# First attention's PSUM: three tiles of two banks in place of six of one

## The chip, the cores and the metric

One Trainium2 core runs the whole program. The metric is the device time of one execution in microseconds; lower is better. Five engines work side by side, each through its own list of instructions in a fixed order: TensorE (PE; its weight loads are shown as PEld), VectorE (DVE), ScalarE (ACT), GpSimd (POOL) and SyncE (SP, which issues the DMA). PSUM, where every matmul writes, has eight banks of 512 fp32 columns on 128 partitions.

## The reference, cut to what matters

Two transformer blocks run one after the other on 2048 tokens of width 1024. The change lies in the attention of the first block, which for each block of 128 queries scores all allowed keys with a small indexer, keeps 256 of them, and attends to these:

```python
def block(i):                       # 128 queries, 16 blocks
    allowed = key_chunk[None, :] <= q_chunk[:, None]
    logits = jnp.einsum('bqhd,bsd->bqhs', qib, ki)              # 8 index heads
    iscore = jnp.einsum('bqhs,bqh->bqs', jax.nn.relu(logits), wib)
    iscore = jnp.where(allowed[None], iscore, -jnp.inf)
    _, idx = lax.top_k(iscore, k_sel)                           # 256 keys
    ...
    s = jnp.einsum('bqgrd,bqkgd->bqgrk', qg, kg) * scale        # 8 heads, 2 key heads
    p = jax.nn.softmax(s, axis=-1)
    o = jnp.einsum('bqgrk,bqkgd->bqgrd', p, vg)
```

Around it stand an input projection, a pooling branch, two gated output projections, and a second block with a windowed attention.

## The kernel before

The program has five stages: the projections that attention needs (`phase_a`), the first attention together with the other 28 projections of the first block (`dense`), the merge of the first block, the second block's projections with its attention, and the second merge. The change touches the second stage.

**Attention in tiles.** Block `i` has `K = 128(i+1)` keys. `index_scores` walks them in chunks of 512 columns: one matmul per index head into a PSUM tile (L462), a relu in place on ACT (L465), and a multiply-add into `score` on DVE (L467, L469). `search` then finds the 256th largest score bit by bit; DVE counts (L483, L484), or ACT counts for spans up to 900 keys (L489), and POOL turns each count into the next threshold (L524, L526). Its tail (L563 to L572, on DVE and POOL) writes a `bias` per key, 0 or -1e30, into the tile `half`. `scores` makes, per head and chunk of 512 keys, two matmuls into a PSUM tile (L628) and one DVE instruction that adds the bias, writes `s` to SBUF and keeps the row's extremum (L632, followed by a read of the accumulator); then ACT takes the exponential over up to 1024 columns (L636). `sums` walks the keys two tiles of 128 at a time: four transposes of `s` (two heads) into a PSUM tile (L650), ACT rounds it to `th` (hi, L655), a matmul with minus identity takes hi off the PSUM tile (L657), ACT rounds the rest (lo, L658), and hi and lo are multiplied with the values into `po` (L664). The last of these matmuls is a mark.

**PSUM.** In this stage one bank (`acc`) takes the dense projections, one (`psO`) takes `po`, and six tiles of one bank (`psS`, also used as `psT`) take index scores, attention scores and transposes in turn. `th` has three buffers.

**Order.** Two attention blocks make a unit of 2048 keys altogether (blocks 8 and 6, 9 and 5, 10 and 4, then 15 alone, 14 and 0, 13 and 1, 12 and 2, 11 and 3, and last 7 alone). While one unit attends, the search of the next and the index scores of the one after run beside it (`attention_1`); the search is marked urgent. A scheduler that runs when the program is built lays out each engine's list. Dense matmuls (L295, 24 per output tile, evacuated by ACT at L209) are held by `paced`: after a lead of `D0` groups each group of three may start only behind a mark, so that they spread evenly over the marks; `SL` is the number of marks by which they run ahead.

Of the kernel before, what the change touches and what calls it, by code (L numbers as in the profile page):

```python
# [45 lines left out]
class Prog:  # L46
# [150 lines left out]
    hl = ()  # L197
    D0, SL = 240, 60
    pace = False
    groups = 0  # L200
    turned = []
    AK = 900
    TP, PP, BP, HW, PO = 3, 5, 3, 8, 1
    PASSES = ((0, 0), (0, 1), (1, 0))
# [53 lines left out]
    def ps(self, pool):  # L258
        return pool.tile([P, 512], F32, name="ps")

# [188 lines left out]
    def index_scores(self, x, i, off):  # L449

        nc = self.nc
        K = (i + 1) * P
        for h0 in (0, 4):
            qI = self.xp.tile([P, 4, P], F32R, name="qI")
            nc.sync.dma_start(qI.bitcast(F32), self.qid[i][:, h0:h0 + 4])
            for c0 in range(0, K, 512):
                w = min(512, K - c0)
                n = max(w, 256)
                xc = x[:, off + c0:off + c0 + w]
                for h in range(h0, h0 + 4):  # L460
                    ps = self.ps(self.psS)
                    nc.tensor.matmul(ps[:, :n], qI[:, h - h0, :], self.kI[:, c0:c0 + n], start=True, stop=True)  # L462
                    wc = self.wi[:, i, h:h + 1]
                    r = ps[:, :w]
                    nc.scalar.activation(r, r, AF.Relu)  # L465
                    if h == 0:
                        nc.vector.tensor_scalar(xc, r, wc, 0.0, op0=ALU.mult, op1=ALU.add)  # L467
                    else:
                        nc.vector.scalar_tensor_tensor(xc, r, wc, xc, op0=ALU.mult, op1=ALU.add)  # L469
                    yield w / 960.0  # L470
        nc.vector.memset(x[0:64, off + K - 64:off + K], -3.0e38)
# [129 lines left out]
    def scores(self, x, g, pr):  # L601
# [11 lines left out]
        for e in range(2):  # L613
# [8 lines left out]
            ss.append(s)  # L622
            for c0 in range(0, K, 512):
                w = min(512, K - c0)
                n = max(w, 256)
                ps = self.ps(self.psS)
                for q in (x["qA"], x["qB"]):
                    nc.tensor.matmul(ps[:, :n], q[:, 2 * pr + e, :], x["kap"](g, c0, n), start=q is x["qA"],  # L628
                                     stop=q is x["qB"])
                first = nm[:, h:h + 1] if c0 else 3.0e38 if sink is None else sink[1][:, h:h + 1]  # L630
# [8 lines left out]
    def sums(self, x, g, pr):  # L639
# [3 lines left out]
        po = self.psO.tile([P, 512], F32, name="po")  # L643
        for k0 in range(0, nkt, 2):
            m = min(2, nkt - k0)
            pt = self.ps(self.psT).rearrange("p (k e t) -> p k e t", k=2, e=2)
            for kk in range(m):
                for e in range(2):
                    c, off = divmod((k0 + kk) * P, self.CW)
                    nc.tensor.matmul(pt[:, kk, e, :], ss[e][c][:, off:off + P], self.ident.bitcast(F32), is_transpose=True,  # L650
                                     start=(kk == e == 0), stop=(kk == m - 1 and e == 1))
            th = self.tp.tile([P, 2, 2, 256], F32R, name="th")
            ptf = pt[:, :m].rearrange("p k e t -> p k (e t)")
            hi, lo = th[:, 0, :m], th[:, 1, :m]
            nc.scalar.copy(hi, ptf)  # L655
            if self.PL == "E":
                nc.tensor.matmul(ptf, self.minus, hi, start=False, stop=True, skip_group_check=True)  # L657
                nc.scalar.copy(lo, ptf)  # L658
# [452 lines left out]
    def run(self):  # L1111
# [28 lines left out]
        with ExitStack() as es:  # L1140
# [5 lines left out]
            with ExitStack() as ep:  # L1146
# [5 lines left out]
                self.projected = self.turned[-76:]  # L1152
            self.banks(es, 1, 7 - self.PO)
            self.psO = self.pl(es, "psO", self.PO, PSUM)
            self.psT = self.psS
            self.att_pools(es, 1024, self.PP, self.TP)
# [125 lines left out]
```

## Time and profile before

| what | us |
|---|---|
| median of 3 runs | 3424.64 (3421.09 to 3427.6) |
| the profiled execution | 3433.52 |
| its span in the trace | 3431.8 |
| PE busy over the span | 3185.6 (93%) |
| DVE busy | 2353.4 (69%) |
| ACT busy | 1862.0 (54%) |

A group of the profile's costliest instructions gives line, engine and operation, what is written from what, the count, the busy time, the mean length of one, and the engine's idle time before them with what ended it. A row of a table by windows gives each engine's busy time in a stretch, with the number of instructions, and then the granted TensorE clock as a share of full speed (1.00 is 2.4 GHz, 0.50 is 1.2 GHz).

### The profile page before, as it was taken

The page shows a single profiled execution, that of the slowest core. Times are in us where ns is not written, and L with a number is a line of the kernel's source. Part 1 is how long each engine was busy: PE and PEld are TensorE (multiplying, and loading weights), DVE is VectorE, ACT ScalarE, POOL GpSimd, SP SyncE. Part 2 cuts the span into 40 slices and gives each one's busy share as a digit, 9 for nine tenths or more (in the row PEclk, how much of TensorE's full clock was granted, in tenths as well). Part 3 has the DMA queues.
Part 4 walks back from the last instruction along what each step waited for, and adds up shares of the span by engine and source line. Part 5 has one row for each costly group of instructions (what it writes and reads, how often), then busy time and mean ns, then how long its engine had stood idle before and what let it go on. Part 6 is the DMA issues. An engine that isn't in the chain of part 4 may idle for free. (4 is left out here: it accounts for less than half of the span.)

```text
span 3431.8 us, 47878 instructions
## 1 busy us (share of the span) xinstructions
PE 3185.6 (93%) x15880; PEld 2642.8 (77%) x15880; DVE 2353.4 (69%) x4745; ACT 1862.0 (54%) x3498; POOL 820.6 (24%) x1293
## 2 busy tenths in 40 slices
PE   5997989999988999997889999999999999999998
PEld 5996767787766777875667878888888887777787
DVE  5875778889998888635887556446446455668765
ACT  3553676886666687663444333335444445764443
POOL 0432145522324365202322113102102111111100
PEclk9998999999988999998899999999999999999999
DMA  5657875435323443566886555445555446878654
GB/s 182 236 159 267 281 263 182 145 127 172 128 76 103 131 150 129 163 196 195 258 280 230 183 173 175 164 154 174 192 152 187 153 149 211 256 223 275 227 184 147
DMA packets 290824, 637.78 MB, mean 186 GB/s; under 512 B 46096, under 2 KB 100112, under 8 KB 276240
## 3 DMA queue, kind: packets, MB, share of 16 engines
q1 hardware_dynamic: 290576, 634.73, 56.7%
q8 instruction: 125, 2.05, 0.2%
q14 instruction: 123, 1.01, 0.1%
HBM read 467.22 MB, written 167.38 MB: 185 GB/s over the span
## 5 line engine op out<-in xcount | busy, mean ns | idle before, releaser
L295 PE MATMUL ps<-h,hl 128*128 128x512 f32 x5376 | 1372.9, 400 | 18.0 <-ACT st L209 16.6
L295 PEld LDWEIGHTS ps<-h,hl 128*128 128x128 f32 x5376 | 987.0, 189 | 227.0 <-ACT st L209 26.8
L274 PE MATMUL ps<-hl,h 128*128 128x512 f32 (+3 forms) x3840 | 821.5, 368 | 27.5 <-DVE st L899 9.8
L274 PEld LDWEIGHTS ps<-hl,h 128*128 128x128 f32 x3840 | 671.1, 191 | 126.2 <-DVE st L899 10.8
L337 DVE TENSOR_TENSOR hl<-raw,hl 128x1024 fp32r<-128x1024 f32 (+3 forms) x364 | 440.6, 1211 | 333.9 <-ACT hl L336 332.2
L336 ACT CAST hl<-raw 128x1024 fp32r<-128x1024 f32 (+4 forms) x380 | 366.4, 965 | 380.0 <-PE ps L274 143.2
L878 PE MATMUL ps<-h,hl 128*128 128x512 f32 x1536 | 384.4, 410 | 29.6 <-DVE g L880 9.2
L878 PEld LDWEIGHTS ps<-h,hl 128*128 128x128 f32 x1536 | 299.7, 197 | 104.9 <-ACT hl L336 11.6
L484 DVE SCALAR_TENSOR_TENSOR junk<-half,sm,junk 128x704 bf16<-128x704 int16 (+17 forms) x316 | 321.9, 1019 | 5.3
L524 POOL TENSOR_SCALAR sm<-sm 128x1 f32<-128x1 f32 x448 | 181.4, 408 | 591.6 <-DVE junk L484 297.4
L636 ACT ACTIVATE s<-s,nm 128x1024 f32<-128x1024 f32 (+7 forms) x320 | 237.7, 745 | 152.9 <-DVE nm L632 151.7
L650 PE MATMUL ps<-ident,s 128*128 128x128 f32 x1344 | 225.3, 279 | 34.1 <-ACT s L636 28.7
L655 ACT CAST th<-ps 128x512 fp32r<-128x512 f32 (+1 forms) x352 | 196.1, 572 | 84.2 <-PE ps L650 60.5
L650 PEld LDWEIGHTS ps<-ident,s 128*128 128x128 f32 x1344 | 167.0, 143 | 72.4 <-ACT s L636 42.1
L664 PE MATMUL po<-th,vS 128*128 128x256 f32 x1088 | 200.6, 290 | 4.0 <-ACT th L658 3.3
L469 DVE SCALAR_TENSOR_TENSOR score<-ps,wi,score 128x512 f32<-128x512 f32 (+3 forms) x266 | 177.6, 679 | 20.9 <-ACT ps L465 18.5
L664 PEld LDWEIGHTS po<-th,vS 128*128 128x128 f32 x1088 | 167.6, 190 | 30.0 <-ACT th L658 11.3
L526 POOL TENSOR_SCALAR sm<-sm 128x1 f32<-128x1 f32 x448 | 180.5, 403 | 40.0
L658 ACT CAST th<-ps 128x512 fp32r<-128x512 f32 (+1 forms) x288 | 156.9, 567 | 56.3 <-PE ps L657 55.1
L465 ACT ACTIVATE ps<-ps 128x512 f32<-128x512 f32 (+3 forms) x304 | 154.3, 534 | 56.1 <-PE ps L462 55.5
L483 DVE TENSOR_SCALAR junk<-half,sm 128x704 bf16<-128x704 int16 (+17 forms) x316 | 145.5, 460 | 48.0 <-POOL sm L526 43.3
L209 ACT COPY st<-ps 128x512 f32<-128x512 f32 x156 | 91.1, 584 | 135.5 <-PE ps L295 69.9
(278 smaller groups left out, 4049.3 us busy)
## 6 DMA issues: line engine op xcount, KB each, us to landing
hl<-wk SPq DMA_DIRECT2D x84, 1024.0 KB, 5.2
raw<-in_wu SPq DMA_DIRECT2D x140, 512.0 KB, 4.4
raw<-in_wd SPq DMA_DIRECT2D x128, 512.0 KB, 4.5
zd<-st SPq DMA_DIRECT2D x224, 256.0 KB, 2.9
g<-zd SPq DMA_DIRECT2D x128, 256.0 KB, 4.4
wk<-hl SPq DMA_DIRECT2D x28, 1024.0 KB, 4.8
qd<-qs SPq DMA_DIRECT2D x32, 512.0 KB, 5.7
qA<-qd SPq DMA_DIRECT2D x64, 256.0 KB, 3.4
```

The lines of the kernel that those rows point to most:

```text
L274: nc.tensor.matmul(ps[b][:, :n], h[k][:, s, b * P:(b + 1) * P], wt[:, r, kk, :], start=(k == 0 and i == 0), stop=(k == KT - 1 and i == 2))
L295: nc.tensor.matmul(ps, wt[:, r, k, :], h[k][:, s, :], start=(k == 0 and i == 0), stop=(k == KT - 1 and i == 2))
L336: self.nc.scalar.copy(hi, src)
L337: (eng or self.nc.gpsimd).tensor_sub(lo, src, hi.bitcast(F32))
L484: self.nc.vector.scalar_tensor_tensor(junk, x[:, h:], thr, junk, op0=op, op1=ALU.add, accum_out=out)
L524: nc.gpsimd.tensor_scalar(one(u, e), one(p, e), one(q, e), 0.5 if bit else 1.0, op0=ALU.is_ge, op1=ALU.subtract)
L526: nc.gpsimd.tensor_scalar(one(c, e), one(u, e), w, one(c, e), op0=ALU.mult, op1=ALU.add)
L636: nc.scalar.activation(p, p, AF.Exp, scale=-1.0, bias=nm[:, h:h + 1], accum_out=x["sums"][:, c, h:h + 1])
L650: nc.tensor.matmul(pt[:, kk, e, :], ss[e][c][:, off:off + P], self.ident.bitcast(F32), is_transpose=True, start=(kk == e == 0), stop=(kk = ...
L655: nc.scalar.copy(hi, ptf)
L664: last = nc.tensor.matmul(po[:, :256], x["vap"](kt, g), th[:, r, kk], start=(kt == 0 and r == 0), stop=(kt == nkt - 1 and r == 1))
L878: nc.tensor.matmul(ps, wt[:, r, 4 * e + k, :], ab[4 * e + k][:, s, :], start=(k == 0 and i == 0), stop=(k == 3 and i == 2))
```

## The change

`psS` becomes three tiles of 1024 columns, that is two banks each. Each matmul still writes 512 columns at most, so a chunk of 1024 keys takes two matmuls (or two pairs) into the halves of one tile; what ACT and DVE do with the tile they do in one instruction of up to 1024 columns. `sums` goes four key tiles at a time: eight transposes, one hi of 1024 columns, two corrections of 512, one lo of 1024. `th` doubles in size and has two buffers in place of three. There are fewer marks (one per four key tiles), and `SL` goes from 60 to 30. The second block's attention keeps its 512 columns.

```diff
-    D0, SL = 240, 60
+    D0, SL = 240, 30
+    wide = None
-    TP, PP, BP, HW, PO = 3, 5, 3, 8, 1
+    TP, PP, BP, HW = 2, 5, 3, 8
...
-        return pool.tile([P, 512], F32, name="ps")
+        return pool.tile([P, 1024 if pool is self.wide else 512], F32, name="ps")
...
-            for c0 in range(0, K, 512):
-                w = min(512, K - c0)
-                n = max(w, 256)
+            for c0 in range(0, K, 1024):
+                w = min(1024, K - c0)
...
-                    nc.tensor.matmul(ps[:, :n], qI[:, h - h0, :], self.kI[:, c0:c0 + n], start=True, stop=True)
+                    for d in range(0, w, 512):
+                        n = max(min(512, w - d), 256)
+                        nc.tensor.matmul(ps[:, d:d + n], qI[:, h - h0, :], self.kI[:, c0 + d:c0 + d + n], start=True, stop=True)
...
-            for c0 in range(0, K, 512):
-                w = min(512, K - c0)
-                n = max(w, 256)
+            for c0 in range(0, K, self.CW):
+                w = min(self.CW, K - c0)
                 ps = self.ps(self.psS)
-                for q in (x["qA"], x["qB"]):
-                    nc.tensor.matmul(ps[:, :n], q[:, 2 * pr + e, :], x["kap"](g, c0, n), start=q is x["qA"],
-                                     stop=q is x["qB"])
+                for d in range(0, w, 512):
+                    n = max(min(512, w - d), 256)
+                    for q in (x["qA"], x["qB"]):
+                        nc.tensor.matmul(ps[:, d:d + n], q[:, 2 * pr + e, :], x["kap"](g, c0 + d, n),
+                                         start=q is x["qA"], stop=q is x["qB"])
...
-        for k0 in range(0, nkt, 2):
-            m = min(2, nkt - k0)
-            pt = self.ps(self.psT).rearrange("p (k e t) -> p k e t", k=2, e=2)
+        step = self.CW // 256
+        for k0 in range(0, nkt, step):
+            m = min(step, nkt - k0)
+            pt = self.ps(self.psT).rearrange("p (k e t) -> p k e t", k=step, e=2)
...
-            th = self.tp.tile([P, 2, 2, 256], F32R, name="th")
+            th = self.tp.tile([P, 2, step, 256], F32R, name="th")
...
-                nc.tensor.matmul(ptf, self.minus, hi, start=False, stop=True, skip_group_check=True)
+                for d in range(0, m, 2):
+                    nc.tensor.matmul(ptf[:, d:min(d + 2, m)], self.minus, hi[:, d:min(d + 2, m)], start=False, stop=True,
+                                     skip_group_check=True)
...
-            self.banks(es, 1, 7 - self.PO)
-            self.psO = self.pl(es, "psO", self.PO, PSUM)
-            self.psT = self.psS
+            self.acc = self.pl(es, "acc1", 1, PSUM)
+            self.psO = self.pl(es, "psO", 1, PSUM)
+            self.psT = self.psS = self.wide = self.pl(es, "psS", 3, PSUM)
```

PE's list holds the same 15800 matmuls before and after. DVE's and ACT's lists are 384 instructions shorter each: on ACT 304 relus become 176, and 576 casts (hi and lo) of this attention become 320; on DVE 304 multiply-adds become 176, and 320 reductions, each with its read of the accumulator, become 192. The lists differ from the first index matmul on; from the merge of the first block onward they hold the same work in the same order, up to a few places near its beginning.

The first place is PE's list where block 15 takes over from blocks 10 and 4 and its first transposes, corrections and products stand. Before (L650 transposes, L657 correction, L664 products with the values, L462 index scores, L628 scores):

```order
L650 MATMUL ps<-ident,s 128x128 x9
L462 MATMUL ps<-kI,qI 128x512
L657 MATMUL ps<-th,minus 128x512
L664 MATMUL po<-th,vS 128x256
L650 MATMUL ps<-ident,s 128x128 x4
L657 MATMUL ps<-th,minus 128x512 x2
L664 MATMUL po<-th,vS 128x256 x4
L628 MATMUL ps<-kS,qA 128x512
L628 MATMUL ps<-kS,qB 128x512
```

and now (L654, L662, L670, L464 and L631 are the same five):

```order
L654 MATMUL ps<-ident,s 128x128 x7
L464 MATMUL ps<-kI,qI 128x512 x2
L654 MATMUL ps<-ident,s 128x128 x8
L662 MATMUL ps<-th,minus 128x512 x2
L670 MATMUL po<-th,vS 128x256
L631 MATMUL ps<-kS,qA 128x512
L631 MATMUL ps<-kS,qB 128x512
```

Two steps of eight transposes now stand one behind the other ahead of the first correction; in between there is no dense matmul in either list.

The second place is PE's list in the middle of the same unit, from a step's transposes to its products. Before:

```order
L650 MATMUL ps<-ident,s 128x128 x4
L295 MATMUL ps<-h,hl 128x512 x3
L628 MATMUL ps<-kS,qA 128x512
L628 MATMUL ps<-kS,qB 128x512
L664 MATMUL po<-th,vS 128x256 x3
L462 MATMUL ps<-kI,qI 128x512
L657 MATMUL ps<-th,minus 128x512
L664 MATMUL po<-th,vS 128x256
```

and now, with the dense matmuls at L296:

```order
L296 MATMUL ps<-h,hl 128x512 x18
L662 MATMUL ps<-th,minus 128x512 x2
L670 MATMUL po<-th,vS 128x256
L464 MATMUL ps<-kI,qI 128x512
L464 MATMUL ps<-kI,qI 128x256
L654 MATMUL ps<-ident,s 128x128 x8
L670 MATMUL po<-th,vS 128x256 x7
```

Work comes in longer runs of one kind: dense matmuls in a run of 18 where runs of three stood, and the next step's eight transposes between a correction and the products that need its lo.

The third place is DVE's list where the search of block 15's unit has just ended and that of blocks 14 and 0 is in its middle. Tile `half_5642` holds the bias of block 15, which is the unit that attends next; `half_6756` and `half_7815` belong to units behind it. Before:

```order
L549 SCALAR_TENSOR_TENSOR half_6756<-half_6756,sm_6759,low_7812 128x1920
L469 SCALAR_TENSOR_TENSOR score_7842<-ps_7867,wi_207,score_7842 128x512
L632 ISA s_7836,nm_7830<-ps_7838,half_5642 128x512
L632 ISA nm_7830 128x1
L537 TENSOR_SCALAR low_7820<-half_7815 128x1792
L553 TENSOR_TENSOR sm_6759<-sm_6759 128x1
```

and now, where `half_4295` is the bias of the unit that still attends (blocks 10 and 4):

```order
L551 SCALAR_TENSOR_TENSOR half_6340<-half_6340,sm_6343,low_7252 128x1920
L635 ISA s_7140,nm_6846<-ps_7141,half_4295 128x640
L635 ISA nm_6846 128x1
L635 ISA s_7157,nm_6846<-ps_7158,half_4295 128x640
L635 ISA nm_6846 128x1
L555 TENSOR_TENSOR sm_6343<-sm_6343 128x1
```

Behind the same instruction of the search (L549, now L551) DVE took up the new unit's first scores; now it has two of the old unit's scores left.

## Rows read from the trace of the kernel before

**Rows 1.** The page's first part: the span, and and per engine the busy time, its share of the span and the instructions.

```profile
span 3431.8 us, 47878 instructions
PE 3185.6 (93%) x15880; PEld 2642.8 (77%) x15880; DVE 2353.4 (69%) x4745; ACT 1862.0 (54%) x3498; POOL 820.6 (24%) x1293
```

**Rows 2.** The views of lines L462 and L664: engine, operation, count, then the shortest, median and longest instruction in ns, then the first and the last start in us.

```profile
L462 PE MATMUL ps<-kI,qI x304: 274/393/796, 336.1 to 1295.8; 128*128 128x512 f32 x112, 128*128 128x256 f32 x24, 128*128 128x384 f32 x16
...
L664 PE MATMUL po<-th,vS x1088: 274/281/416, 572.2 to 1555.7; 128*128 128x256 f32 x182
```

**Rows 3.** Busy time by windows over the stage of the first attention: window, its length, then for PE, PEld, DVE, ACT and POOL the busy us with the number of instructions, the granted TensorE clock, the share of the DMA engines, GB/s. The last row sums the four.

```profile
320.00:560.00 240.00, 222.51 (x921) 171.87 (x920) 176.36 (x357) 149.25 (x281) 81.09 (x195) 0.98 0.75 260
560.00:920.00 360.00, 346.36 (x1862) 287.26 (x1861) 316.73 (x732) 277.38 (x588) 129.04 (x294) 0.99 0.44 148
920.00:1220.00 300.00, 258.59 (x1313) 209.45 (x1312) 265.87 (x582) 199.65 (x413) 107.58 (x200) 0.90 0.31 100
1220.00:1560.00 340.00, 328.60 (x1853) 275.99 (x1852) 225.67 (x585) 241.63 (x526) 118.92 (x244) 1.00 0.52 166
sum 1240.00, PE 1156.06 PEld 944.57 DVE 984.63 ACT 867.90 POOL 436.64; mean PE 289.01 PEld 236.14 DVE 246.16 ACT 216.98 POOL 109.16
```

**Rows 4.** What PE waited for from 320 to 1560 us: the waiting line and the one that released it, us in total, times, longest.

```profile
PE ps L295 <- ACT st L209: 16.4, 24, 2.0
PE ps L462 <- DVE score L469: 15.5, 8, 8.2
PE ps L650 <- ACT s L636: 14.4, 13, 3.5
...
PE ps L657 <- ACT th L655: 7.1, 5, 5.2
PE ps L628 <- DVE nm L632: 6.6, 8, 1.7
PE ps L650 <- DVE nm L632: 3.9, 2, 3.0
PE po L664 <- ACT th L658: 3.3, 7, 0.7
```

**Rows 5.** The table by windows again (columns as in rows 3), for two stretches inside units and four short ones at their changes.

```profile
840.00:920.00 80.00, 79.72 (x462) 68.84 (x461) 75.23 (x170) 58.21 (x130) 18.41 (x55) 1.00 0.44 140
940.00:960.00 20.00, 9.90 (x20) 5.13 (x21) 19.37 (x48) 8.81 (x13) 2.30 (x3) 0.52 0.00 1
...
1060.00:1080.00 20.00, 13.98 (x53) 9.27 (x51) 16.84 (x36) 9.53 (x14) 9.54 (x6) 0.85 0.20 73
1080.00:1100.00 20.00, 15.77 (x76) 12.17 (x76) 18.95 (x47) 18.70 (x42) 9.32 (x25) 0.81 0.21 66
1180.00:1200.00 20.00, 14.48 (x70) 11.70 (x69) 14.87 (x43) 11.05 (x26) 5.52 (x4) 0.83 0.49 155
...
1340.00:1400.00 60.00, 60.00 (x351) 51.97 (x351) 49.18 (x134) 43.62 (x97) 33.02 (x60) 1.00 0.43 137
```

**Rows 6.** ACT's groups of instructions by line and shape, 320 to 1560 us: line, engine, operation, what is written from what, count, then busy us, mean ns of one, idle time before them and who ended it.

```profile
L655 ACT CAST th<-ps 128x512 fp32r<-128x512 f32 x256 | 146.8, 594 | 46.3 <-PE ps L650 24.5 <-PE po L664 21.1
L658 ACT CAST th<-ps 128x512 fp32r<-128x512 f32 x256 | 145.4, 591 | 53.8 <-PE ps L657 52.6
L465 ACT ACTIVATE ps<-ps 128x512 f32<-128x512 f32 x224 | 126.8, 587 | 42.7 <-PE ps L462 42.3
...
L655 ACT CAST th<-ps 128x256 fp32r<-128x256 f32 x32 | 12.1, 377 | 3.4 <-PE po L664 1.7 <-PE ps L650 1.6
```

**Rows 7.** DVE's groups by line and shape over the same stretch, columns as in rows 6.

```profile
L469 DVE SCALAR_TENSOR_TENSOR score<-ps,wi,score 128x512 f32<-128x512 f32 x196 | 145.0, 745 | 16.9 <-ACT ps L465 15.9
L632 DVE CUSTOM_DVE_ANT_0 s<-ps,half,nm 128x512 f32<-128x512 f32 x120 | 89.4, 746 | 32.0 <-PE ps L628 23.4 <-PE ps L650 7.0 <-issue 0.2
...
L632 DVE DVE_READ_ACCUMULATOR2_ANT nm<- 128x1 f32 x320 | 26.3, 82 | 0.0
...
L469 DVE SCALAR_TENSOR_TENSOR score<-ps,wi,score 128x256 f32<-128x256 f32 x21 | 10.0, 478 | 0.3 <-ACT ps L465 0.3
```

**Rows 8.** The timeline near 338 us, where six relus and three multiply-adds run without a gap: start in us, us from the first start to the last end, engine, line, operation, shape, count.

```profile
337.81 3.03 ACT L465 ACTIVATE ps<-ps 128x512 f32<-128x512 f32 x6
...
341.27 2.06 DVE L469 SCALAR_TENSOR_TENSOR score<-ps,wi,score 128x512 f32<-128x512 f32 x3
```

**Rows 9.** The timeline at the change from blocks 10 and 4 to block 15, in order of start; columns as in rows 8, and in brackets the engine's wait before the instruction and who ended it.

```profile
937.70 4.05 POOL L572 TENSOR_TENSOR half<-half,eq 128x2048 bf16<-128x2048 bf16 x1
...
938.33 3.69 DVE L483 TENSOR_SCALAR junk<-half,sm 128x960 bf16<-128x960 int16 x1
...
938.71 0.40 PE L628 MATMUL ps<-kS,qB 128*128 128x512 f32 x1
...
944.33 2.22 DVE L549 SCALAR_TENSOR_TENSOR half<-half,sm,low 128x1920 uint16<-128x1920 int16 x1 [0.60 <-ACT low L547]
946.47 0.74 DVE L469 SCALAR_TENSOR_TENSOR score<-ps,wi,score 128x512 f32<-128x512 f32 x1
...
947.27 0.79 PE L462 MATMUL ps<-kI,qI 128*128 128x512 f32 x1 [8.16 <-DVE score L469]
...
955.01 0.47 PE L650 MATMUL ps<-ident,s 128*128 128x128 f32 x1 [1.81 <-ACT s L636]
```

More of the change, by code (lines that the diff above doesn't have):

```diff
@@ L650, in sums @@
                     nc.tensor.matmul(pt[:, kk, e, :], ss[e][c][:, off:off + P], self.ident.bitcast(F32), is_transpose=True,
-                                     start=(kk == e == 0), stop=(kk == m - 1 and e == 1))
-            th = self.tp.tile([P, 2, 2, 256], F32R, name="th")
+                                     start=(kk % 2 == e == 0), stop=(e == 1 and (kk % 2 == 1 or kk == m - 1)))
+            th = self.tp.tile([P, 2, step, 256], F32R, name="th")
             ptf = pt[:, :m].rearrange("p k e t -> p k (e t)")
```

## The prediction

> **What bounds the kernel now.** I read the first part of the page, then the tables by windows over the changed stage, then PE's waits there, and last the timeline at one bad place. The page shows PE busy for 3185.6 of 3431.8 us [rows 1], so a gain has to come out of PE's idle time or out of its clock. The changed work runs from the first index matmul at 336 us to the last product with the values at 1556 us [rows 2]. From 320 to 1560 us PE is busy for 1156.1 of 1240 us, DVE for 984.6, ACT for 867.9 [rows 3]: 84 us of PE idleness. The clock column adds to that: 0.98 over 240 us, 0.99 over 360 and 0.90 over 300 mean 4.8, 3.6 and 30 us lost, 38 us together. No change that leaves PE's work alone can give more than 84 + 38 = 122 us here.
>
> The reader should see where this sits. Inside a unit PE is full: 79.7 of 80 us from 840, with DVE at 75.2, and 60.0 of 60 from 1340, with DVE at 49.2 [rows 5]. The loss sits at the changes of unit: 10.1 us of PE idleness from 940 to 960 at a clock of 0.52, then 6.0, 4.2 and 5.5 us in the stretches at 1060, 1080 and 1180, at 0.85, 0.81 and 0.83 [rows 5]. That is 25.8 us of idleness and (0.48 + 0.15 + 0.19 + 0.17) x 20 = 19.8 us of clock, 45.6 us in 80. The clock is at full speed in the full stretches and falls in those with pauses; it follows the waits.
>
> At 938.7 us PE had run out of what it may start. Its next index matmul waited 8.16 us for a PSUM tile to be freed by a multiply-add on DVE, and DVE reached this at 946.5, behind search work: a count of 3.69 us beside POOL's 4.05 us product, and a 2.22 us instruction that waited for ACT [rows 9]. After that the new unit has to fill up: its first transpose comes at 955.0 [rows 9]. Dense matmuls could not fill the pause, since they wait for marks and no mark falls there.
>
> **The change part by part.** *PE* keeps its 15800 matmuls of the same shapes: 0.
>
> *ACT* drops 384 instructions. Casts of 512 and 256 columns take 594 and 377 ns [rows 6], so 256 columns cost 217 ns and the fixed part is 160 ns; 384 x 0.16 = 61 us by duration. Six relus without a gap take 3.03 us [rows 8], so they start (3.03 - 0.587) / 5 = 0.49 us apart with the relu's 587 ns [rows 6]; 512 columns are 0.434 of that, and a merged pair frees only 0.055 us: 21 us. *DVE* drops 256 instructions and 128 reads of the accumulator. Multiply-adds of 512 and 256 columns take 745 and 478 ns [rows 7]: fixed part 211 ns, so 54 us, with 128 x 0.082 = 10 us more for the reads. Three in a row take 2.06 us [rows 8], so they start 0.66 apart, of which 0.534 are columns: 0.125 x 256 = 32 us. I take the spacing, 21 and 32 us, since it is what the next instruction sees. The Trainium skill (Perfetto Trace Analysis, Optimizing Scalar/DVE Operations) says that grouping into larger operations helps if the engine is saturated, and gives about 51 ns per ScalarE and 125 ns per VectorE instruction on PSUM, with about twice that in the profiled latency. By its figures the sum is 20 and 32 us, by our durations it would be 61 and 64; our spacing sides with the page.
>
> Neither engine is the bound inside a unit, where PE is full [rows 5]; what DVE saves there is hidden behind PE and worth nothing. It counts at the changes of unit. The refill there is made of reductions and multiply-adds in a row, and a pair of 1.33 us becomes 1.20: about 1 us in each refill. More may come from the order. In the new list two of the old unit's scores still stand behind the search's instruction that was followed by the new unit's first scores, so at that change the search comes earlier against the attention, and the old unit can cover its tail. Bounds: 0, because the pieces in DVE's way in rows 9 are the search's own, and 45.6 us, all that these four stretches lose. I take 15 us: the 8.2 us wait at 938.7, half of the 9.6 us of clock behind it, and 2 us for two refills. That is the value nearest to the one row whose cause the order touches.
>
> *Handing over.* The chain from transposes to products grows: eight transposes in place of four, two casts of 594 + 434 = 1028 ns in place of 594, two corrections in place of one. There are 160 such steps in place of 288. Before, PE waited 7.1 us for hi and 3.3 us for lo [rows 4]. Scaled by length and count, 10.4 x 1028 / 594 x 160 / 288 = 10.0 us: no change. But work now comes in longer runs of one kind, and where two steps stand back to back the cover is thinner. Bounds: a gain of 10 us (these waits vanish, since ACT has more room), and a loss of 46 us, if one cast in three of the 320 shows its whole extra 0.434 us. I take a loss of 5 us, near the scaled row.
>
> *Tiles.* Six tiles of 512 or three of 1024 hold the same 3072 columns, but PE can only take a whole one. Before, it waited for DVE to free score, index and transpose tiles for 15.5 + 6.6 + 3.9 = 26 us, 8.2 of it at 938.7 [rows 4]. Queued behind such a wait stands all of PE's list, dense matmuls too. Bounds: a gain of 10 us (DVE is quicker through its list), a loss of 26 us (the waits double). I take 0. The two wide th buffers hold eight key tiles where three held six; ACT idled 21.1 us for a free one [rows 6], off PE's path: 0. The dense lead is 30 of 160 marks in place of 60 of 288, or 19 and 21 per cent: 0.
>
> Sum on the profiled execution: 3433.5 - 15 + 5 = 3423.5 us. It lies 8.9 us above the median of the runs, so the median becomes about 3424.6 - 10 = **3414.6 us**.
>
> **The rivals.** *A: three tiles are too few.* This ends on the other side. PE's list is fixed, and with three tiles it can run at most two whole tiles ahead of ACT and DVE. One tile held by a transpose step through both casts, one waiting for DVE behind a count, and PE stops with dense work queued behind the stopped matmul. For it speak the pauses that exist already with six tiles (26 us on DVE, 10.4 us on casts [rows 4]), and the new list, which puts two steps of eight transposes and four score matmuls into three tiles with no dense matmul between. Against it speaks that DVE and ACT have more slack than before. Price: casts +25 us (half of the upper bound), tiles +15 (a little more than half), and the 15 us at the changes still won: 3424.6 + 25 = about 3450 us. It decides as soon as PE's own work between a step's last transpose and its correction is often shorter than ACT's queue plus 1.03 us. The Trainium skill (Perfetto Trace Analysis, Optimizing Tensor Performance, Matmuls) has a rule on this side: independent matmul groups should rotate through different PSUM banks so that the evacuation of one overlaps the next group's matmuls. Here a group occupies two banks at a time and three groups rotate where six did; by that rule the result is rival A's.
>
> *B: it cancels.* PE is full inside units and the pause at 938.7 is the search's own. Then 15 us shrink to 5 and the handing over takes them back: 3424 us. For it speaks that the longest pieces in rows 9 are untouched.
>
> *C: the changes of unit heal.* The search comes early everywhere and three quarters of the 45.6 us go, and the clock stays up: 3424.6 - 35 + 0 = 3390 us. Against it speaks that the refill, from the first scores to the first transpose (947 to 955 us in rows 9), remains a chain through DVE and ACT with no marks in it.
>
> That the change doesn't do what it says is no case: the lists carry the 384 fewer instructions on each of the two engines.
>
> **How the numbers follow.** Forecast, 3405 to 3417 us: 0.34. C, below 3405: 0.09. B, 3418 to 3431: 0.24. A, above 3431: 0.33. Of A a tenth of all chance lies above 3455, of C some 0.06 below 3385, so the range is 3385 to 3455. The cases of both signs hold most of the chance, so the forecast's own range stands beside it: 3405 to 3417. Faster by over 0.2% (6.8 us, about what a measurement of this kernel can tell from no change) are the forecast and C, 0.43; within 0.2% is B, 0.24; slower is A, 0.33.
>
> **What would show it.** Relus, casts and reductions of 1024 columns near 1.03 us on ACT and 1.28 us on DVE; busy time in the stage down by some 20 us on ACT and 32 on DVE, with PE's unchanged. If I am right, the stretch near 940 us loses its 8 us wait and the low clock behind it, and PE's waits for casts stay near 15 us. If A is right, PE's waits at the correction and the products exceed 30 us in the stage, or those for DVE exceed 40, and PE is no longer full inside units. If B is right, the wait for the multiply-add near 940 us is there again, at its length. The prediction is wrong from the ground if the stage after 1560 us moves, where the lists are the same.

## The result, and the profile after

The change made the kernel slower. The median of four runs is 3469.12 us (3465.47 to 3473.7) against 3422.86 us of the kernel before (3419.67 to 3427.6, four runs): a ratio of 1.013, 95% interval 1.0111 to 1.0148, or +46 us. The forecast of 3414.6 us had the wrong sign, and the time lies above the range.

The profiled execution after took 3465.47 us, 32 us more than the one before (3433.52). The two stand on different sides of their medians, 10.7 us above and 3.7 us below; that makes up the 46.

The page's first part after, to be read beside [rows 1]:

```profile
span 3463.7 us, 46985 instructions
...
PE 3189.3 (92%) x15880; PEld 2641.7 (76%) x15880; DVE 2331.6 (67%) x4361; ACT 1836.6 (53%) x3114; POOL 816.9 (24%) x1293
```

PE's busy time grew by 4 us, the span by 32. DVE and ACT have 384 instructions fewer each, as the lists said. The last product with the values now starts at 1590.9 us where it started at 1555.7 [rows 2]: the stage is 35 us longer, and the work behind it takes 3 us less. The windows over the stage, with columns as in [rows 3] (the last window is 40 us longer than there):

```profile
320.00:560.00 240.00, 222.50 (x926) 172.73 (x925) 162.08 (x295) 144.54 (x229) 77.47 (x192) 0.99 0.76 264
560.00:920.00 360.00, 323.94 (x1723) 264.52 (x1722) 306.42 (x590) 256.87 (x432) 138.33 (x300) 1.00 0.41 133
920.00:1220.00 300.00, 264.71 (x1361) 215.91 (x1361) 257.13 (x464) 189.93 (x311) 94.60 (x179) 0.95 0.34 110
1220.00:1600.00 380.00, 354.69 (x1947) 294.42 (x1947) 234.74 (x522) 250.92 (x449) 125.42 (x265) 0.99 0.48 154
sum 1280.00, PE 1165.85 PEld 947.59 DVE 960.38 ACT 842.27 POOL 435.82; mean PE 291.46 PEld 236.90 DVE 240.09 ACT 210.57 POOL 108.95
```

PE's idle time is the window less the first number. It was 17.5, 13.6, 41.4 and 11.4 us before [rows 3] and is 17.5, 36.1, 35.3 and 25.3 now. The window with the bad change of unit, 920 to 1220, gained 6 us, and its clock rose from 0.90 to 0.95. The two windows that were nearly full lost 22 and 14. The short stretches say the same:

```profile
840.00:920.00 80.00, 74.64 (x410) 61.23 (x409) 75.65 (x136) 54.34 (x85) 20.49 (x55) 1.00 0.34 108
940.00:960.00 20.00, 16.52 (x83) 13.33 (x82) 14.90 (x33) 12.22 (x19) 4.16 (x5) 0.91 0.35 107
1340.00:1400.00 60.00, 58.06 (x327) 48.63 (x326) 53.09 (x129) 41.50 (x75) 35.30 (x78) 1.00 0.37 114
```

From 940 to 960 PE does 83 matmuls where it did 20, at a clock of 0.91 in place of 0.52 [rows 5]: the 8 us wait of [rows 9] is gone, and no wait of PE in the stage is longer than 4.7 us. A part of it lives on under another name, as these lines of PE, ACT and DVE show (columns as in [rows 9]):

```profile
941.58 0.93 PE L654 MATMUL ps<-ident,s 128*128 128x128 f32 x7
945.93 0.58 PE L670 MATMUL po<-th,vS 128*128 128x256 f32 x1 [3.43 <-ACT th L664]
...
943.63 1.99 ACT L549 ACTIVATE low<-score,sm 128x1920 uint16<-128x1920 uint16 x1 [5.81 <-DVE sm L546]
945.53 0.35 ACT L664 CAST th<-ps 128x256 fp32r<-128x256 f32 x1
...
939.32 4.02 DVE L485 TENSOR_SCALAR junk<-half,sm 128x960 bf16<-128x960 int16 x1
```

The cast to lo stands in ACT's list behind an instruction of the search (L549), for which ACT waits 5.81 us while DVE counts; PE's row calls it a wait of 3.43 us for lo.

But the stretches inside units, where PE was busy for 79.7 of 80 us and 60.0 of 60, now hold 5.4 and 1.9 us of idleness. PE's waits from 320 to 1610 us, columns as in [rows 4]:

```profile
PE po L670 <- ACT th L664: 24.8, 26, 3.4
PE ps L296 <- ACT st L210: 21.1, 27, 3.0
PE ps L662 <- ACT th L659: 10.3, 16, 1.6
PE ps L654 <- ACT s L639: 10.0, 8, 2.0
PE ps L631 <- DVE nm L635: 9.6, 7, 4.3
PE ps L654 <- DVE score L471: 8.6, 8, 3.0
PE ps L654 <- DVE nm L635: 5.6, 11, 1.3
PE ps L631 <- DVE score L471: 5.0, 3, 3.5
PE ps L654 <- DVE sm L534: 4.7, 1, 4.7
PE ps L464 <- DVE nm L635: 4.3, 6, 1.3
PE ps L464 <- DVE score L471: 3.8, 1, 3.8
```

The products wait 24.8 us for lo and the corrections 10.3 us for hi, 35.1 together in place of 10.4 [rows 4]. PE's waits for DVE, with their small rows, are 43.0 us in place of 31.7 (1.4 and 5.7 us of this in rows that are not shown), and those for the evacuation of the dense tiles 21.1 in place of 16.4. Waits for exponentials fell from 14.4 to 10.0 us, and those of index matmuls for the load of `qI` to 0.4 us, from this row of before:

```profile
PE ps L462 <- DMA qI<-qid: 7.7, 3, 3.9
```

Together that is 29 us more, which is nearly all of the idleness that PE gained (83.9 us before, 114.2 now).

The rows name ACT and DVE, but neither got busier: ACT's busy time fell from 867.9 to 842.3 us and DVE's from 984.6 to 960.4. Their instructions have the lengths that the prediction worked out (1028 and 1279 ns), as the groups by shape show, columns as in [rows 6]:

```profile
L659 ACT CAST th<-ps 128x1024 fp32r<-128x1024 f32 x112 | 113.0, 1014 | 64.3 <-PE ps L654 61.3 <-PE po L670 2.7
L664 ACT CAST th<-ps 128x1024 fp32r<-128x1024 f32 x112 | 111.8, 1013 | 33.9 <-PE ps L662 33.7
...
L471 DVE SCALAR_TENSOR_TENSOR score<-ps,wi,score 128x1024 f32<-128x1024 f32 x70 | 89.6, 1280 | 11.7 <-ACT ps L467 11.0
```

ACT sat idle for 61.3 us ahead of the first cast because PE's transposes had not come (24.5 in [rows 6]), so PE waits for ACT and ACT for PE. The two `th` buffers are not what is short: ACT's idle time for one, behind products, fell from 21.1 us [rows 6] to 2.7. The timeline shows how a wait for lo comes about, first PE, then ACT (columns as in [rows 9]):

```profile
1023.49 0.62 PE L662 MATMUL ps<-th,minus 128*128 128x512 f32 x2
1023.95 0.28 PE L670 MATMUL po<-th,vS 128*128 128x256 f32 x1
1024.07 1.03 PE L654 MATMUL ps<-ident,s 128*128 128x128 f32 x8
1026.54 1.10 PE L670 MATMUL po<-th,vS 128*128 128x256 f32 x7 [1.44 <-ACT th L664]
...
1023.73 1.14 ACT L639 ACTIVATE s<-s,nm 128x1024 f32<-128x1024 f32 x1
...
1024.87 0.68 ACT L467 ACTIVATE ps<-ps 128x640 f32<-128x640 f32 x1
1025.49 1.00 ACT L664 CAST th<-ps 128x1024 fp32r<-128x1024 f32 x1
```

The corrections end at 1024.1 us, but lo is begun 1.4 us later, since an exponential and a relu stand ahead of it in ACT's list, and then takes 1.00 us. PE has only the next step's eight transposes to do meanwhile, and stands for 1.44 us. The pause here is one for data, in the order of the lists; no free tile is waited for. A second pause inside a unit, PE first, then one line of DVE:

```profile
844.31 0.39 PE L631 MATMUL ps<-kS,qA 128*128 128x512 f32 x1
...
845.24 0.62 PE L464 MATMUL ps<-kI,qI 128*128 128x512 f32 x2
845.69 0.33 PE L631 MATMUL ps<-kS,qA 128*128 128x384 f32 x1
845.86 0.34 PE L631 MATMUL ps<-kS,qB 128*128 128x384 f32 x1
848.10 0.33 PE L654 MATMUL ps<-ident,s 128*128 128x128 f32 x1 [1.90 <-ACT s L639]
848.32 0.74 PE L464 MATMUL ps<-kI,qI 128*128 128x512 f32 x2
...
845.44 1.22 DVE L635 CUSTOM_DVE_ANT_0 s<-ps,half 128x1024 f32<-128x1024 f32 x1
```

Score, index and score matmuls take three tiles from 844.3 to 846.2. Then the next thing in the list is a transpose, which waits for an exponential, and PE stands for 1.90 us at full clock. DVE had read the first of the three tiles by 846.7, so this too is a wait for data: index matmuls stand behind the transpose in the list, and no dense matmul starts from 844.1 to 855.9. Over the stage the waits for exponentials fell; those that grew are the ones for lo, for DVE, for hi and for the dense evacuation. How far the order of the lists comes from the three tiles is what the experiments have to show.

### The profile page after: what moved, and what is told of

It is laid out like the page before. It is cut to its first block, busy times and chain, and to the rows that moved or that the text cites. A ratio compares the mean times of both kernels' runs of the same rounds, so it can differ in the third digit from the quotient of the medians.

```text
span 3463.7 us, 46985 instructions
## 1 busy us (share of the span) xinstructions
PE 3189.3 (92%) x15880; PEld 2641.7 (76%) x15880; DVE 2331.6 (67%) x4361; ACT 1836.6 (53%) x3114; POOL 816.9 (24%) x1293
## 5 line engine op out<-in xcount | busy, mean ns | idle before, releaser
L296 PE MATMUL ps<-h,hl 128*128 128x512 f32 x5376 | 1358.9, 400 | 23.5 <-ACT st L210 21.3
L296 PEld LDWEIGHTS ps<-h,hl 128*128 128x128 f32 x5376 | 989.4, 190 | 241.7 <-ACT st L210 34.0
L275 PE MATMUL ps<-hl,h 128*128 128x512 f32 (+3 forms) x3840 | 820.2, 367 | 23.0 <-DVE st L905 10.3
L884 PEld LDWEIGHTS ps<-h,hl 128*128 128x128 f32 x1536 | 299.0, 197 | 107.3 <-DVE hl L338 10.4
L486 DVE SCALAR_TENSOR_TENSOR junk<-half,sm,junk 128x704 bf16<-128x704 int16 (+17 forms) x316 | 323.4, 1024 | 7.1
L654 PE MATMUL ps<-ident,s 128*128 128x128 f32 x1344 | 210.1, 281 | 42.8 <-ACT s L639 23.3
L659 ACT CAST th<-ps 128x1024 fp32r<-128x1024 f32 (+3 forms) x224 | 178.2, 799 | 114.8 <-PE ps L654 108.4
L654 PEld LDWEIGHTS ps<-ident,s 128*128 128x128 f32 x1344 | 163.9, 144 | 76.6 <-ACT s L639 36.7
L670 PE MATMUL po<-th,vS 128*128 128x256 f32 x1088 | 183.7, 291 | 25.8 <-ACT th L664 24.8
L670 PEld LDWEIGHTS po<-th,vS 128*128 128x128 f32 x1088 | 152.8, 191 | 51.8 <-ACT th L664 41.3
L635 DVE CUSTOM_DVE_ANT_0 s<-ps,half 128x1024 f32<-128x1024 f32 (+7 forms) x128 | 126.0, 986 | 73.3 <-PE ps L631 67.4
L471 DVE SCALAR_TENSOR_TENSOR score<-ps,wi,score 128x1024 f32<-128x1024 f32 (+7 forms) x154 | 156.6, 1019 | 25.5 <-ACT ps L467 23.5
L664 ACT CAST th<-ps 128x1024 fp32r<-128x1024 f32 (+3 forms) x160 | 139.1, 884 | 53.3 <-PE ps L662 53.1
```

Of the source, the lines that this page charges most:

```text
L275: nc.tensor.matmul(ps[b][:, :n], h[k][:, s, b * P:(b + 1) * P], wt[:, r, kk, :], start=(k == 0 and i == 0), stop=(k == KT - 1 and i == 2))
L296: nc.tensor.matmul(ps, wt[:, r, k, :], h[k][:, s, :], start=(k == 0 and i == 0), stop=(k == KT - 1 and i == 2))
L486: self.nc.vector.scalar_tensor_tensor(junk, x[:, h:], thr, junk, op0=op, op1=ALU.add, accum_out=out)
L670: last = nc.tensor.matmul(po[:, :256], x["vap"](kt, g), th[:, r, kk], start=(kt == 0 and r == 0), stop=(kt == nkt - 1 and r == 1))
L884: nc.tensor.matmul(ps, wt[:, r, 4 * e + k, :], ab[4 * e + k][:, s, :], start=(k == 0 and i == 0), stop=(k == 3 and i == 2))
```

## The experiments

Four theories were set against each other. **U**: tiles are short; each use takes one whole and gives it back whole, so the list cannot put other work between a step's parts. **T**: the casts are too long (1.03 us between transposes and products). **W**: wide instructions on ACT and DVE hold up what is queued behind them. **P**: marks that are twice as far apart spread the dense matmuls badly. A measure for U is the number of uses that one tile must serve: 304 index chunks, 320 score chunks and 288 steps make 912 before, or 152 for each of six tiles; 176 + 192 + 160 = 528 now, or 176 for each of three.

| kernel | tiles | uses of each | ratio to before (95%) | us |
|---|---|---|---|---|
| the change | 3 wide | 176 | 1.013 (1.0111 to 1.0148) | +46 |
| e5, before with five tiles | 5 narrow | 182 | 1.011 (1.0092 to 1.0128) | +38 |
| e9, before with four | 4 narrow | 228 | 1.0307 (1.0291 to 1.0322) | +107 |
| e3, before with three | 3 narrow | 304 | 1.0734 (1.0706 to 1.0762) | +248 |
| e1, steps of two key tiles | 3 wide | 219 | 1.0484 (1.0466 to 1.0502) | +163 |
| e2, chunks of 512 keys | 3 wide | 261 | 1.0505 (1.0482 to 1.0528) | +170 |
| e4, scores wide, steps narrow | 2 wide, 2 narrow | 184, 144 | 1.0219 (1.0194 to 1.0245) | +71 |
| e8, marks twice as dense | 3 wide | 176 | 1.0195 (1.018 to 1.021) | +67 |
| e7, casts in halves | 3 wide | 176 | 1.0267 (1.0248 to 1.0287) | +90 |
| e6, all reads in halves | 3 wide | 176 | 1.0358 (1.0338 to 1.0377) | +123 |
| e10, relu to SBUF | 6 narrow | 152 | 1.0039 (1.0024 to 1.0054) | +14 |
| e11, the same, five tiles | 5 narrow | 182 | 1.011 (1.0095 to 1.0125) | +39 |
| e12, the change, relu to SBUF | 3 wide | 176 | 1.0307 (1.0287 to 1.0328) | +103 |

The microseconds are differences of medians with the runs of before on the same chip.

**e1: the steps go by two key tiles again**, in half of a wide tile, with three th buffers and the old marks; scores stay wide.

```diff
-    D0, SL = 240, 30
+    D0, SL = 240, 60
-    TP, PP, BP, HW = 2, 5, 3, 8
+    TP, PP, BP, HW = 3, 5, 3, 8
-        step = self.CW // 256
+        step = 2
-            pt = self.ps(self.psT).rearrange("p (k e t) -> p k e t", k=step, e=2)
+            pt = self.ps(self.psT)[:, :512].rearrange("p (k e t) -> p k e t", k=step, e=2)
```

> Scores stay wide in three tiles of 1024 columns; the sums go back to two key tiles a step (casts of 512, three th buffers, 288 marks, lead of 60), and a transpose step uses half of a wide tile. Theory T (the long step of the sums is what costs: its casts of 1.01 us stand behind too little PE work): PE's waits for hi and lo, 35 us in the changed kernel, fall to 10 to 15 us, and the time falls to 3420 to 3435 us. Theory U (three whole tiles are too few, whatever is in them): PE's waits for DVE to free tiles stay at 40 us or more, and the time stays at 3455 us or above.

Measured 3592.02 us, +163. Casts of half the length and more marks did not help; PE's waits for lo rose to 40.8 us and for hi to 22.4. U's expectation came true, T's did not: a tile that is half used is taken like a whole one.

**e2: index and attention scores go by 512 keys again**, each chunk in half of a wide tile; the steps stay at four key tiles (`CW` in the second loop, 1024 in the first).

```diff
-            for c0 in range(0, K, 1024):
-                w = min(1024, K - c0)
+            for c0 in range(0, K, 512):
+                w = min(512, K - c0)
```

> Index scores and scores go back to chunks of 512 columns, each in half of a wide tile; the sums keep their four key tiles a step. Theory T: PE's waits for hi and lo stay above 30 us, and the time stays at 3455 to 3475 us. Theory U: the tiles now hold half as much, so PE's waits for DVE rise beyond the 42 us of the changed kernel, and the time rises to 3480 us or more. If neither holds and it is the wide DVE instructions that cost, the time falls to 3435 us or below.

Measured 3598.77 us, +170. As in e1, the half of the work that went back to narrow pieces made the time longer, not shorter, as U expected: each piece still takes a wide tile.

**e3: the kernel before with three tiles of 512**, nothing else changed (`PO` is 1).

```diff
-            self.banks(es, 1, 7 - self.PO)
+            self.banks(es, 1, 3)
```

> The kernel before with three PSUM tiles of 512 columns in place of six, nothing else changed. Theory T: the step of the sums is short, so the time stays within 10 us of the kernel before, 3423 to 3433 us. Theory U: three tiles are too few, and with half of the columns they are worse than the change: 3470 us or more, with PE's waits for DVE above 42 us.

Measured 3676.72 us, +248. PE's waits, with the old lines and casts of 512 columns:

```profile
PE po L664 <- ACT th L658: 35.6, 57, 2.7
PE ps L657 <- ACT th L655: 25.4, 45, 1.5
PE ps L650 <- DVE nm L632: 19.5, 28, 3.1
PE ps L628 <- DVE nm L632: 19.3, 26, 5.4
```

The waits for lo and hi are 61 us with the short casts, where six tiles have 10.4 [rows 4]. Waits at the casts can thus come from a shortage of tiles alone; they need no long cast. T falls as the sole cause.

**e4: two wide tiles for scores, two narrow ones for the steps.** Here the steps go by two key tiles, with three th buffers and `SL = 60` as in e1.

```diff
-            self.psT = self.psS = self.wide = self.pl(es, "psS", 3, PSUM)
+            self.psS = self.wide = self.pl(es, "psS", 2, PSUM)
+            self.psT = self.pl(es, "psT1", 2, PSUM)
```

> Six banks as two wide tiles for index scores and scores and two narrow ones for transposes; sums by two key tiles with three th buffers, 288 marks and a lead of 60. Theory T: the cover of the casts is back and DVE and ACT keep part of their savings: 3410 to 3430 us, PE's waits for hi and lo near 10 us. Theory U: two tiles for scores are fewer still, so PE's waits for DVE exceed 42 us and the time is 3465 us or more.

Measured 3500.21 us, +71. This is 92 us better than e1, whose instructions are the same: four tiles in place of three, of the same six banks. It is still behind the change; the products wait 47.0 us for lo, now that two tiles are all that the steps have. U's time came true and its sign did not: PE's waits for DVE at these tiles are 37.2 us, not over 42.

**e5: the kernel before with five tiles** (`banks(es, 1, 5)`).

> The kernel before with five PSUM tiles of 512 columns in place of six (one bank unused). Theory U, as it stands now (PE's list is short of PSUM; a tile taken and given back whole makes three of 1024 worth about five of 512): 3455 to 3490 us, about the time of the changed kernel, with PE's waits for lo and hi above 20 us in the stage though the casts are of 512 columns. Theory T (the length of the casts): within 10 us of the kernel before, 3420 to 3435 us.

Measured 3462.96 us, +38. PE's waits from 320 to 1600 us:

```profile
PE ps L295 <- ACT st L209: 24.2, 29, 4.1
PE po L664 <- ACT th L658: 12.9, 20, 2.4
PE ps L650 <- ACT s L636: 11.7, 15, 1.9
...
PE ps L657 <- ACT th L655: 4.6, 7, 1.5
```

One tile fewer, with nothing else changed, costs nearly as much as the whole change. The waits for lo and hi are 17.5 us, more than with six tiles (10.4) but less than the 20 that U expected. The six tiles of before were not in excess.

**e6: the changed kernel with every read in two halves of 512**: relus, multiply-adds, reductions and both casts. For the casts:

```diff
-            nc.scalar.copy(hi, ptf)
+            halves = [slice(d, min(d + 2, m)) for d in range(0, m, 2)]
+            for d in halves:
+                nc.scalar.copy(hi[:, d], ptf[:, d])
...
-                nc.scalar.copy(lo, ptf)
+                    nc.scalar.copy(lo[:, d], ptf[:, d])
```

> The changed kernel with its three full tiles of 1024 columns, but every relu, multiply-add, reduction and cast on them done in two pieces of 512; tiles, steps, marks and th as in the change. Theory U: a tile is still taken and freed whole, so the time stays at 3455 to 3490 us. Theory W (the wide instructions themselves hold up the first half of their tile): back to 3420 to 3440 us.

Measured 3548.31 us, +123 against before and 77 more than the change. That is above U's range too. The tiles are the same as in the change, and reading them in halves does not bring the time back; W falls. The wide instructions are worth at most the 77 us, since a part of it is a side effect: the second correction now also waits for the first lo (17.1 us of PE's waits).

The Trainium skill (Perfetto Trace Analysis, Optimizing Scalar/DVE Operations) says that breaking up instructions may let work complete sooner if these engines are not saturated but cause bubbles on others. Here the bubbles are there and the engines are not full, and the halves cost time in e6 and e7, with the side effect in both. U's reason, that a whole tile comes free only with its second half, is argued and not shown.

**e7: only the casts in halves**, the same lines as above.

> The changed kernel with hi and lo of each step of four key tiles rounded in two casts of 512 columns, so that a correction starts behind its own half; all else as in the change. Theory T: PE's waits for hi and lo fall from 35 to 15 us and the time to 3440 to 3450 us. Theory U: these waits are what the list shows where no tile is free for other work, so they may fall, but the time stays at 3458 to 3480 us.

Measured 3515.47 us, +90. It has the same side effect (9.5 us of waits of the second correction for the first lo), so it is no clean test of the length of a cast. The waits for lo and hi are 37.0 us (18.6 and 12.8, and 5.6 of products for a hi), where the change has 35.1, and the time is 44 us longer. Neither T's range nor U's came true.

**e8: marks at every second key tile**, as many as before, with `SL = 60`.

```diff
-            self.marks.append(last.ins)
+                if kk % 2 == 1 or kk == m - 1:
+                    self.marks.append(last.ins)
```

> The changed kernel with a mark after every second key tile and a lead of 60 marks, so that the dense matmuls are let go as finely as before. Theory P (dense work comes in runs that are too long to cover the casts): 3430 to 3450 us, with PE's waits for lo below 12 us. Theories T and U: 3458 to 3480 us.

Measured 3492.02 us, +67. Finer marks make it 21 us worse than the change; P falls. It is above the range of T and U too, which let the marks do nothing: another order of the list alone can move the time by some 20 us.

**e9: the kernel before with four tiles** (`banks(es, 1, 4)`).

> The kernel before with four tiles of 512 in place of six; all instructions keep their length, th its three buffers, the marks their number. It fills the gap between five tiles (+38 us) and three (+248). Theory U (the time follows how many uses each tile must serve): 928 / 4 = 232 uses of each tile, between the runs with 224 (+163) and 248 (+248), though these served wide tiles in part; from five and three narrow tiles alone the value would lie nearer the lower, since the cost grows faster than the shortage: 3535 to 3605 us. Rival (some other property of three tiles is what costs, a step that cannot be kept two ahead): four tiles cost little more than five, 3465 to 3490.

Measured 3536.44 us, +107, at the lower end of what U gave. PE's waits for lo and hi from 320 to 1850 us are 34.1 us:

```profile
PE po L664 <- ACT th L658: 24.6, 35, 2.8
...
PE ps L657 <- ACT th L655: 9.5, 15, 1.5
```

Six, five, four and three tiles cost 0, 38, 107 and 248 us with the same instructions: each tile that goes costs more than the one before it. (The expectation counted 928 uses, with 16 small ones for the sums; the table leaves these out.)

**e10: the kernel before with the relu written to SBUF** (a pool `rp` of two buffers), which frees the PSUM tile before DVE's multiply-add.

```diff
-                    r = ps[:, :w]
-                    nc.scalar.activation(r, r, AF.Relu)
+                    r = self.rp.tile([P, 512], F32, name="r")[:, :w]
+                    nc.scalar.activation(r, ps[:, :w], AF.Relu)
```

> The kernel before, with the relu of the index scores written to an SBUF tile of 512 columns (two buffers) in place of back into its PSUM tile. The PSUM tile is free after the relu and no longer waits for the multiply-add on DVE. Theory U: the wait of the index matmuls for DVE (15.5 us before, 8.2 of it at one place) goes, and some of the others with it: 3400 to 3420. Rival (six tiles are enough, the long wait was only the place where the search showed itself): 3420 to 3430. A second rival on the other side: DVE's multiply-adds now read two SBUF operands and hold up POOL, or two relu buffers hold up ACT: above 3435.

Measured 3443.1 us, +14: the second rival, by both of its signs. PE no longer waits for a multiply-add, but ACT's relus wait 23.7 us for one of the two buffers, DVE's multiply-adds of 512 columns take 805 ns in place of 745 [rows 7], and POOL's 448 pairs of one-column steps of the search are longer, 464 and 449 ns on average in place of 408 and 403. The timeline of e10 shows where; first DVE, then POOL:

```profile
861.76 0.74 DVE L469 SCALAR_TENSOR_TENSOR score<-r,wi,score 128x512 f32<-128x512 f32 x1
...
861.94 0.71 POOL L524 TENSOR_SCALAR sm<-sm 128x1 f32<-128x1 f32 x1 [1.65 <-DVE junk L484]
```

and the same pair in the kernel before:

```profile
848.13 0.74 DVE L469 SCALAR_TENSOR_TENSOR score<-ps,wi,score 128x512 f32<-128x512 f32 x1
...
848.32 0.28 POOL L524 TENSOR_SCALAR sm<-sm 128x1 f32<-128x1 f32 x1 [1.81 <-DVE junk L484]
```

With both operands in SBUF, DVE's instruction keeps POOL's step until it is over, 0.71 us in place of 0.28. Which of the three makes the 14 us was not separated.

**e11: e10 with five tiles** (`banks(es, 1, 5)`).

> The same with five tiles of 512. Theory U: the shorter hold of the 304 index uses makes up for most of the missing tile: of the +38 us of five tiles at least 20 come back, 3420 to 3443. Rival (the number of tiles costs by itself, however long each is held): 3455 to 3470.

Measured 3468.0 us, +39: in the rival's range, U's expectation missed. From e10 to e11 the loss of the sixth tile costs 25 us, where it costs 38 without the edit. That fits a shorter hold, but the losses of e10 are in both, so it is not shown.

**e12: the changed kernel with the relu written to an SBUF tile of 1024 columns**, one buffer, with `PP` (buffers of s) from five to four.

> The changed kernel with the relu written to an SBUF tile of 1024 columns (one buffer; the buffers of s fall from five to four to make room). The three wide tiles are free after the relu. Theory U: some of the +46 us comes back, 3425 to 3455. Rival (index tiles are not what is short, the steps of eight transposes are): 3465 to 3485. One relu buffer may make the relus wait for DVE, which would show as a wait of ACT on the multiply-add and could bring it above.

Measured 3531.88 us, +103, above both ranges. POOL's steps take 495 and 490 ns, in place of 407 and 403 in the change; ACT's relus wait 52.7 us for the one buffer to be read by DVE's multiply-adds, which is the sign that the expectation named for a time above:

```profile
ACT r L467 <- DVE score L471: 49.8, 27, 6.4
...
ACT r L467 <- DVE score L469: 2.9, 4, 1.1
```

How much of the 57 us beyond the change is POOL, how much the fourth buffer of s and how much the one of r was not separated.

## Why the prediction was wrong

**The step that failed is *Tiles*, taken at 0, and with it *Handing over*, taken at 5 us.** *Tiles* counted columns: six tiles of 512 and three of 1024 hold the same 3072. It left out how often a whole tile is used and given back. The change merges pairs, so the uses fall, but not to half (912 to 528, since short chunks and steps do not pair), while the tiles do fall to half: 152 uses of each become 176. With unchanged instructions, 182 uses of each cost 38 us (e5). The bound of 26 us, the doubling of the waits for DVE in [rows 4], is below that as well, since it took the rows' names for causes. A shortage shows itself under other names too, as waits for hi and lo: 17.5, 34.1 and 61.0 us with five, four and three tiles.

***Handing over*** measured 24.7 us (35.1 less 10.4), most of the 29 us by which PE's waits grew. The scaling by length and count was not what set it; e5, e9 and e3 show such waits rising from fewer tiles alone. But the five tiles of e5, with 182 uses of each, give 17.5 us of them, and the change, with 176, gives twice that. So a shortage of the size of e5's does not account for all of it, and how much the longer steps and the order of ACT's list add stays open.

**PE 0** held: the stage's busy time went from 1156.1 us to 1160.9 between 320 and 1595, the same matmuls. (Both traces hold 15880 on PE, 80 more than the 15800 of the prediction.)

**ACT and DVE** had the sizes right: 1014 ns for a cast and 1280 for a multiply-add, busy time in the stage 26 us less on ACT (21 forecast) and 24 on DVE (32 forecast). **The gain at the changes of unit** had the right place and was too big at 15 us. The 8.2 us wait went, but 3.4 us of idleness at the same place came as a wait for lo, and from 920 to 1220 the idleness fell by 6 us where 10 were taken. For the clock 4.8 us were taken; PE's busy time per matmul in that window fell from 0.197 us (258.59 for 1313) to 0.194 (264.71 for 1361), some 3 us, an estimate, since the shapes are not quite the same.

**Rival A** was the case that came true, by its own signs: 35.1 us of waits at correction and products (over 30), 43.0 us of waits for DVE (over 40), PE no longer full inside units. The Trainium skill (Perfetto Trace Analysis, Optimizing Tensor Performance, Matmuls) asks that independent groups rotate through different PSUM banks; the result fell on its side, but it says nothing of how many tiles are enough. Rival A's price of +25 us was still too low, since it kept 15 us of gain at the changes and set tiles at 15. Its chance of 0.33 was second to the forecast's 0.34.

What is shown: fewer tiles with equal instructions cost 38, 107 and 248 us; four tiles in place of three, of the same six banks, gain 92 (e4 against e1); narrow pieces in wide tiles cost 163 and 170; finer marks and halved reads, these with a side effect, do not bring the time back. What is argued: that the 46 us of the change are this same shortage, less what the wide instructions give back. PSUM is full, so wide reads on as many tiles as before could not be run, and the two parts cannot be separated in the change itself. A rival that no run separates is the coarser order: the pieces from which the lists are laid out are twice as long in the change, e1 and e2 make them short again only together with more uses of each tile, and e8 moved the time by 21 us with tiles and instructions unchanged. The table also shows that uses of each tile are no law: e1 at 219 costs more than e9 at 228. A wide use lasts longer, and how much length of hold counts beside number stays open; e10 to e12 were meant for that and brought POOL's loss and ACT's waits for a buffer with them.

## What to carry to other kernels

Where an engine runs a fixed list through a pool of PSUM tiles, price a regrouping by the uses that one tile must serve, not by columns (a guide and no law, as e1 beside e9 shows), and measure the slope first: one tile taken from the pool, a one-line edit, cost 38 us here and would have shown that the pool had nothing to spare. A wait for a cast or a reduction whose engine is itself idle for want of the waiting engine, as ACT was for 61 us here, can be a sign of too little work in flight: e3, with casts of half the length and half as many tiles as before, had more of such waits than the change. Look then at what stands ahead of the cast in its engine's list. Here the wide instructions did not pay for the tiles that they cost.

## What the hardware showed unexpectedly

A one-column step on POOL took 0.71 us beside a 0.74 us multiply-add of DVE that reads two SBUF operands, and 0.28 us beside the same multiply-add when it reads PSUM and SBUF. The Trainium skill (GPSIMD Engine Reference, Specifications) states that GpSimd shares its SBUF interfaces with VectorE, with contention for DVE instructions with two SBUF inputs; these rows agree. Writing a result to SBUF to free PSUM early thus has a price on a third engine, here 46 us of POOL's busy time in a search that others wait for (207.1 + 201.2 us in place of 181.4 + 180.5).
